# Mixture of experts on one core: four experts at a time with 32 token slots, weights in 8 KB pieces

## The chip, the cores and the metric

The kernel runs on one core of one Trainium2 chip. The metric is device time in microseconds (us), the median of three runs. TensorE (PE in the profile) multiplies matrices, VectorE (DVE) and ScalarE (ACT) do element-wise work and copies out of the accumulators (PSUM), SyncE (SP) issues the transfers, and 16 DMA engines carry them between the chip's memory and the on-chip memory (SBUF). 1 MB stands for 1,048,576 bytes where loads are counted; the profile's GB/s are 10^9 bytes a second.

## The reference

Two transformer blocks on 256 tokens of 1024 features, everything in float32. The change touches the last part only, a mixture of 32 experts in four groups of eight:

```
g_idx = argmax(xf @ w_router_group)                 # one of 4 groups for each token
top_logit, top_idx = top_k(local[g_idx], 2)         # two of the group's 8 experts
gate  = softmax(top_logit) * g_w                    # g_w: the group's softmax weight
hid   = silu(xblk @ w1[e]) * (xblk @ w3[e])         # w1, w3: 1024 x 512 for each expert
y    += gate * (hid @ w2[e])                        # w2: 512 x 1024 for each expert
out   = x + y                                       # xf, xblk: the tokens after an RMS norm
```

Each token goes to two experts, so there are 512 places over 32 experts. All 32 experts' weights are read: 32 x 3 x 2 MB = 192 MB. On the reference's own inputs the experts get between 4 and 32 tokens; the one with 32 is expert 27, and the token that comes closest to being the 33rd misses by 0.07 in a logit whose standard deviation is 4.8.

## The kernel before

The first five sixths of the program (two mixers, two feed-forwards, a gating unit and a cross attention) are not changed. For the experts the kernel routes the tokens first: it finds group and experts on VectorE, numbers the tokens of each expert (`rk`), and makes one-hot matrices (`select`, L1361) that map 128 slots to tokens: two experts with 64 slots (`CAP`) each.

The loop over pairs (L1532) then does, for each pair:

- `load_in` and `load_out` (L1394, L1409) ask for the pair's weights: 12 loads of 1 MB, each a slot of 128 partitions x 4 x 512 float32. A load takes four chunks of 128 rows, so each partition gets four separate rows of 2 KB.
- `hidden` (L1421): 8 steps over the 1024 features for w1 and then for w3; in each step one product for each expert, the expert's 64 slots as the stationary operand (64 columns of the PE array, the form 128*64 in the profile) and its weights as the moving one (512 columns). The program's product of float32 shows as two instructions in the trace.
- `gated` and `turned` (L1436, L1444): silu, product, and four transposes.
- the gather and the scatter matrix of the next pair (L1380, L1477), products of 128 x 128.
- `outputs` (L1453): products with w2, again 64 columns for each expert, a copy, and at L1457 the scatter back to the tokens, summed in PSUM over all experts.

The weights lie in 22 slots of 1 MB, used in turn (`slots`, L1320; `wslot`): 

```
slots[:] = [ra] * 4 + [rw] * 5 + [wp] * 2 + [cw] * 3 + [wp] * 4 + [(gp, "uh"), (gp, "ul"), rw, (cp, "h")]
```

A load waits until the last product that reads its slot is done, and for the load issued eight before it on the same queue: SP's is the only queue, and the framework keeps eight completion semaphores in turn. The order on each engine is made by a scheduler, except where `keep` pins it. The last pair loads in halves of 1 MB and cuts w2 into four column ranges, so that the end is short.

Two other loads serve below as a measure: at the program's start `u_row` (L502, L504) loads 128 rows of 1024 columns (4 KB each) and 128 rows of 2048 columns (8 KB each):

```
nc.sync.dma_start(wm[:, g, :], A["modT"][g, k * P:k * P + P, :])
nc.sync.dma_start(ws[k][:, 0, :], A["a_w_in"][k * P:k * P + P, 0:2048])
```

If an expert has more than `CAP` tokens, a loop behind a branch (L1568) runs over all experts again, once for each further `CAP` places up to 256.

Of the kernel before, what the change touches and what calls it, by code (L numbers as in the profile page):

```python
# [23 lines left out]
P = 128  # L24
# [7 lines left out]
CAP = 64  # L32

# the order in which some parts are interleaved, one letter for each step
WHOLE = (1, 5)  # rows of the first products for v and g that go in the tensor engine's exact float32
ROW_SEQ = ("rss", "srs", "srrs", "srs")  # layer 0: r the next row's norm, s the split of its weights
BAND_SEQ = ("m", "mm", "mm", "mm", "mm", "xx", "xx", "xx", "yyyy", "yyyx")  # m memory keys, x and y the output's halves
GATE_SEQ = "ghvut0123"  # the gating unit: see todo
CROSS_SEQ = "p1q0x1x21yyx3xy2y233"  # p and q the last queries, 0 to 3 a stage of a head, x and y the output's halves
GATHER_SEQ = (3, 1, 0, 0, 2, 1, 1, 1)  # the first experts: steps of the gather before and between those of w1  # L40
# [51 lines left out]
def _build(ctx, tc, nc, A, out, dbg):  # L92
# [17 lines left out]
    # ---------------------------------------------------------------- constants  # L110
# [41 lines left out]
    # ---------------------------------------------------------------- helpers  # L152
# [72 lines left out]
    def tick():  # L225
        """after each step of a product: a part of the previous one's epilogue, a share of the modulation rows"""
# [9 lines left out]
    def steps_t(w, u, ps, n=512, ks=range(KC)):  # L236
        """w 8 chunks [128, n] stationary, u (hi, lo) [128, 8, 256] moving -> n / 256 banks [128, 2, 256]"""
# [9 lines left out]
    def steps_n(w, u, ps, n=512, whole={}):  # L247
        """u (hi, lo) [128, 8, 256] stationary, w 8 chunks [128, n] moving -> 2 banks [128 tokens, n]"""
# [36 lines left out]
    def inv_rms(ss, n, w=T, eps=0, pool=None, keep=lambda i: i):  # L285
        """(ss / n + eps) ** -0.5 for ss [128, w] in PSUM: the table's value and a Newton step"""
# [43 lines left out]
    def put_u(u, k, src, gain, r, shift=None, keep=lambda i: i):  # L330
        """u[:, k] = src * gain * r + shift, as hi + lo"""
# [17 lines left out]
    # ---------------------------------------------------------------- modulation vectors  # L349
# [18 lines left out]
    def mod_queue(g, gain=None):  # L368
        """in steps for tick()"""
# [17 lines left out]
    def mod_done(g, gain=None):  # L387
        """bias; with a gain: gain * (1 + value)"""
# [7 lines left out]
    def residual(kk, ps, gate=None):  # L396
        """two feature chunks: h += ps * gate"""
# [15 lines left out]
    def norm(outs, adds):  # L413
        """outs: list of (gain(k), shift(k) or None, u)"""
# [5 lines left out]
    # ---------------------------------------------------------------- memory keys and values  # L420
# [22 lines left out]
    def mem_k_steps(hd):  # L443
        """the normalized memory keys of one head, transposed"""
# [17 lines left out]
    def mem_v(c, pool=pb):  # L462
        """256 columns of the memory values"""
# [15 lines left out]
    # ---------------------------------------------------------------- layer 0: HGRN2 mixer  # L479
    # The first norm and the products for f and q go by rows of the weights, each as soon as its modulation is there.  # L480
# [17 lines left out]
    def u_row(k):  # L498
        """the first norm's row k and the weights' row, in steps"""
# [22 lines left out]
    def w_split(n):  # L522
        """the n-th piece of the weights, 512 columns of row n // 4: f first; in steps"""
# [24 lines left out]
    with tc.tile_pool(name="hgrn", bufs=1, reuse_waits="tile") as hp:  # L548
        # lower bound: cumulative sum of the softmax over the single layer, less its first term
# [54 lines left out]
        def widen(lv, hf):  # L604
            """from level lv to level 2 lv"""
# [140 lines left out]
    # ---------------------------------------------------------------- feed-forward  # L746
# [51 lines left out]
    # ---------------------------------------------------------------- layer 1: chunk band attention  # L798
    with tc.tile_pool(name="band", bufs=1, reuse_waits="tile") as bp:
# [37 lines left out]
        def pair(j):  # L837
            """heads 2 j and 2 j + 1: the scores, the probabilities, the output"""
# [89 lines left out]
    # ---------------------------------------------------------------- second block: attention and gating unit  # L928
    with tc.tile_pool(name="blk2", bufs=1, reuse_waits="tile") as bp:
        # both norms at once: h / rms(h) * fin, and that over its own rms:  # L930
        # its mean square is mean(h^2 fin^2) / (mean(h^2) + eps), so that the two together are
        # h fin (mean(h^2 (fin^2 + eps)) + eps^2) ** -0.5
# [46 lines left out]
        def x1_update():  # L979
            """the residual stream enters this block through the first one's final norm"""  # L980
# [6 lines left out]
        def ug_steps():  # L987
            """the gating unit's u, transposed, and its g"""
# [25 lines left out]
        def pair(j):  # L1014
            """heads j and j + 4 of the queries, one for each key head"""
# [129 lines left out]
        # the rows of the attention's features first  # L1145
# [16 lines left out]
    # ---------------------------------------------------------------- memory cross attention  # L1162
# [19 lines left out]
    iota = kconst(mc, "iota")  # L1182
    rw = ctx.enter_context(tc.tile_pool(name="moe_r", bufs=6, side="right", reuse_waits="tile"))
# [17 lines left out]
    def head(hd):  # L1201
        """in three stages: the probabilities, these transposed, the output"""
# [61 lines left out]
    # the router's logits, tokens as rows, without the tokens' 1 / rms, which leaves the order of the experts as it  # L1264
    # is; the tokens themselves as rows, with the sums of their squares
# [65 lines left out]
    # its two experts: the other groups' logits count as -1e30  # L1331
# [13 lines left out]
    # the sum over the experts stays in PSUM, on top of the residual stream  # L1345
# [8 lines left out]
    # the place of each token in its experts' lists, from 1; 0 elsewhere  # L1354
# [5 lines left out]
    def select(es):  # L1360
        """[128 tok, 2, a pair of experts, CAP] one-hot"""  # L1361
        gsel = gp.tile([P, 2, 2, CAP], F32, tag="rms_v256", name=uid("gsel"))
        for tt in range(2):
            nc.vector.tensor_tensor(gsel[:, tt], rk[:, tt, es, None].to_broadcast([P, 2, CAP]),
                                    iota[:, None, 1:CAP + 1].to_broadcast([P, 2, CAP]), op=ALU.is_equal)
        return gsel

    gsel = select(slice(0, 2))
# [10 lines left out]
    # the tokens lack the norm so far: its gain comes to those gathered, 1 / rms to their products  # L1379
    def gather(gsel, g):  # L1380
        """the inputs of a pair of experts, in steps of g chunks"""
        xe = [gp.tile([P, 4, P], F32, tag="sq", name=uid("xe"), bufs=2) for _ in range(2)]
        yield [x[:, k, :] for x in xe for k in range(4)]
        for k0 in range(0, KC, g):
# [5 lines left out]
            for k in range(k0, k0 + g):  # L1390
                nc.scalar.activation(xe[k // 4][:, k % 4, :], ps[:, k - k0, :], AF.Copy, scale=col("nf2", k))
            yield

    def load_in(src, n=4):  # L1394
        """src(name, e): the weights w1 and w3 of a pair of experts, as 8 chunks [128, 512], n at a time"""
        w = {}
        for nm in ("w1", "w3"):
            for kh in range(2):
                ts = [wslot(512) for _ in range(2)]
                for k in range(0, 4, n):  # L1400
                    for e in range(2):
                        k0 = (4 * kh + k) * P
                        nc.sync.dma_start(ts[e][:, k:k + n, :], src(nm, e)[k0:k0 + n * P].rearrange("(k p) n -> p k n", p=P))
                for e in range(2):
# [4 lines left out]
    def load_out(src, cuts=(0, 512, D)):  # L1409
# [226 lines left out]
```

## Time and profile before

| | us |
|---|---|
| median of three runs (1391.45 to 1393.92) | 1392.39 |
| span of the profiled execution | 1390.3 |
| expert stage, from PE's first expert product (905.1) to the end | 485 |
| PE busy in the span | 1360.2 (98%) |
| DMA queue of SP, share of 16 engines' span | 82.0% |
| moved | 408.20 MB, mean 294 GB/s |

The span runs from the first to the last instruction of the profiled execution. That execution's time beyond its span is not in the profile; the median of the runs is 2.1 us above the span, and this is taken as what lies around it. A busy PE is an engine that has matmuls in flight, not one at its peak. The DMA share is the time that packets took on 16 engines; it can go a little over 1, since packets overlap.

### The profile page before, as it was taken

How to read it: one execution, taken by the hardware profiler on the slowest of the kernel's cores; microseconds unless marked ns; L12 is line 12 of the kernel's file. 1: busy time of each engine (PE TensorE's matmuls, PEld its weight loads, DVE VectorE, ACT ScalarE, POOL GpSimd, SP SyncE). 2: the span in 40 equal slices, each digit the busy share in tenths (PEclk: the TensorE clock that was granted, in tenths of full speed). 3: DMA queues.
4: the chain of work that ended last, by engine and by line, in shares of the span. 5: the costliest groups of instructions: out<-in, count | busy, mean ns of one | idle time of the engine just before them, and what ended most of it. 6: DMA issues, size and time to landing. Idle time of an engine off the chain costs nothing. (4 is left out here: it accounts for less than half of the span.)

```text
span 1390.3 us, 24824 instructions
## 1 busy us (share of the span) xinstructions
PE 1360.2 (98%) x9800; PEld 1046.7 (75%) x9800; DVE 734.3 (53%) x1597; ACT 609.2 (44%) x1276; POOL 11.9 (1%) x36
## 2 busy tenths in 40 slices
PE   7999899999999999999999999999999999999997
PEld 6967899999989789999998899954445444445443
DVE  7999998888897767555578777410000000000000
ACT  6756474555665656555577666421111111111111
POOL 2000000000000000000000000000000000000000
PEclk9999999999999999999999999999999999999999
DMA  9958889999878368554154278899999999999997
GB/s 370 377 193 296 284 307 331 328 341 346 316 260 317 124 214 260 188 193 156 62 160 158 72 273 309 291 333 386 387 387 386 386 387 387 387 387 386 387 386 251
DMA packets 219898, 408.20 MB, mean 294 GB/s; under 512 B 9985, under 2 KB 77825, under 8 KB 218754
## 3 DMA queue, kind: packets, MB, share of 16 engines
q1 hardware_dynamic: 219778, 406.58, 82.0%
q8 instruction: 78, 1.28, 0.4%
q14 instruction: 42, 0.34, 0.1%
HBM read 403.39 MB, written 3.15 MB: 292 GB/s over the span
## 5 line engine op out<-in xcount | busy, mean ns | idle before, releaser
L191 ACT ACTIVATE whi<-w 128x512 fp32r<-128x512 f32 (+1 forms) x448 | 277.7, 626 | 234.5 <-PE ps L197 113.9
L192 DVE TENSOR_TENSOR wlo<-w,whi 128x512 fp32r<-128x512 f32 (+1 forms) x448 | 298.6, 682 | 103.9 <-ACT whi L191 103.2
L1428 PE MATMUL r<-w,xe 128*64 128x512 f32 x1024 | 227.4, 596 | 0.0
L198 PE MATMUL ps<-uh,wlo 128*128 128x256 f32 x768 | 216.0, 282 | 1.7 <-DVE wlo L192 1.5
L197 PE MATMUL ps<-ul,whi 128*128 128x256 f32 x768 | 215.7, 281 | 0.5 <-DVE ul L340 0.5
L196 PE MATMUL ps<-uh,whi 128*128 128x256 f32 x768 | 215.6, 281 | 0.0
L1441 DVE SCALAR_TENSOR_TENSOR hs<-r,sc,hs 128x512 f32<-128x512 f32 (+1 forms) x17 | 12.1, 719 | 353.3 <-PE r L1428 353.0
L1428 PEld LDWEIGHTS r<-w,xe 128*64 128x64 f32 x1024 | 70.3, 137 | 136.6 <-issue 133.6
L196 PE MATMUL acc<-uh,whi 128*128 128x256 f32 x592 | 167.4, 289 | 4.7 <-ACT uh L515 4.3
L198 PE MATMUL acc<-uh,wlo 128*128 128x256 f32 x592 | 166.1, 284 | 0.8 <-DVE wlo L192 0.8
L197 PE MATMUL acc<-ul,whi 128*128 128x256 f32 x592 | 166.6, 283 | 0.0
L198 PEld LDWEIGHTS ps<-uh,wlo 128*128 128x128 f32 x768 | 144.5, 188 | 3.1 <-DVE wlo L192 3.1
L197 PEld LDWEIGHTS ps<-ul,whi 128*128 128x128 f32 x768 | 144.7, 188 | 0.7 <-DVE ul L340 0.7
L196 PEld LDWEIGHTS ps<-uh,whi 128*128 128x128 f32 x768 | 144.7, 188 | 0.0
L366 DVE SCALAR_TENSOR_TENSOR mt<-mt,cb 128x1024 f32<-128x1024 f32 x96 | 116.7, 1218 | 23.0 <-DMA mt<-in_modT 23.0
L196 PEld LDWEIGHTS acc<-uh,whi 128*128 128x128 f32 x592 | 110.7, 190 | 8.5 <-ACT uh L515 5.3
L1468 PE MATMUL r<-w,hT 128*64 128x512 f32 (+1 forms) x544 | 113.9, 570 | 0.1
L198 PEld LDWEIGHTS acc<-uh,wlo 128*128 128x128 f32 x592 | 111.7, 189 | 2.1 <-DVE wlo L192 1.2
L197 PEld LDWEIGHTS acc<-ul,whi 128*128 128x128 f32 x592 | 112.2, 190 | 1.3 <-issue 1.0
L196 PE MATMUL acc<-hh,whi 128*128 128x256 f32 x352 | 98.4, 279 | 0.0
L198 PE MATMUL acc<-hh,wlo 128*128 128x256 f32 x352 | 98.3, 279 | 0.0
L197 PE MATMUL acc<-hl,whi 128*128 128x256 f32 x352 | 98.1, 279 | 0.0
(343 smaller groups left out, 1940.9 us busy)
## 6 DMA issues: line engine op xcount, KB each, us to landing
w<-in_w SPq DMA_DIRECT2D x180, 1024.0 KB, 14.2
mt<-in_modT SPq DMA_DIRECT2D x96, 512.0 KB, 5.6
w<-in_ffn_w_in SPq DMA_DIRECT2D x88, 512.0 KB, 5.8
w<-in_ffn_w_out SPq DMA_DIRECT2D x22, 1024.0 KB, 8.4
w<-in_a_w_in SPq DMA_DIRECT2D x16, 1024.0 KB, 9.0
w<-in_w SPq DMA_DIRECT2D x24, 512.0 KB, 11.1
w<-in_modT SPq DMA_DIRECT2D x16, 512.0 KB, 9.0
w<-in_kv_w SPq DMA_DIRECT2D x8, 1024.0 KB, 7.7
```

Source lines behind the costliest of these rows:

```text
L191: keep(nc.scalar.activation(hi, raw, AF.Copy))
L192: keep(nc.vector.tensor_sub(lo, raw, hi.bitcast(F32)))
L196: nc.tensor.matmul(o, lh, rh, start=first, stop=False, skip_group_check=True)
L197: nc.tensor.matmul(o, lh, rl, start=False, stop=False, skip_group_check=True)
L198: nc.tensor.matmul(o, ll, rh, start=False, stop=last, skip_group_check=True)
L366: keep(nc.vector.scalar_tensor_tensor(w, w, 1.0, cb, op0=ALU.mult, op1=ALU.mult, accum_out=modr[:, g, j:j + 1]))
L1428: keep(nc.tensor.matmul(hps[i][e * 64:e * 64 + 64, :], xe[k][:, e * 64:e * 64 + 64], w[nm, e, k], start=k == 0, stop=k == KC - 1))
L1441: nc.vector.scalar_tensor_tensor(hs[:, o:o + n], hps[1][:, o:o + n], rs, hs[:, o:o + n], op0=ALU.mult, op1=ALU.mult)
L1468: keep(nc.tensor.matmul(yp[e * 64:e * 64 + 64, :], hT[:, c, e * 64:e * 64 + 64], w[e, o // 512, c][:, o % 512:o % 512 + n], start=c == 0, ...
```

## The change

Experts are taken four at a time (`G = P // CAP` = 4) with 32 slots each, so that the loop has 8 passes and not 16; each product with weights has 32 stationary columns in place of 64 (form 128*32). Each load of w1 and w3 now takes 512 consecutive rows of an expert, four consecutive rows (8 KB) to a partition; w2 comes in two loads of 1 MB for each expert, two whole rows of 1024 (8 KB) to a partition. So that the products still match, the features are dealt to the partitions in the same way: the token rows are copied with a stride of four (`row_copy`), the gate's output is written so too (`gated`), and the norm's gain comes in that order from `nf2p`, 8 new loads of 32 x 4 single values. The last group loads w1 and w3 as 4 KB pieces and w2 in three column ranges instead of four (2 KB, 1 KB and 1 KB pieces). Comments and docstrings are gone, and lines are numbered anew.

```diff
-CAP = 64
+CAP = 32
+G = P // CAP
+LAST_CUTS = (0, 512, 768, D)
...
+    nf2p = mc.tile([P, KC], F32, name="nf2p")
+    for half in range(2):
+        for q in range(4):
+            src = A["cols"]
+            nc.sync.dma_start(nf2p[32 * q:32 * q + 32, 4 * half:4 * half + 4],
+                              bass.AP(tensor=src.tensor, offset=src.offset + COLS["nf2"][0] + 4 * half + q,
+                                      ap=[[4 * NCOL, 32], [NCOL, 4]]))
...
-        nc.scalar.activation(xg[half, tt], rows[half, tt], AF.Copy)
+        nc.scalar.activation(xg[half, tt].rearrange("t (j p) -> t j p", j=4),
+                             rows[half, tt].rearrange("t (p j) -> t j p", j=4), AF.Copy)
...
-                ts = [wslot(512) for _ in range(2)]
+                ts = [wslot(512) for _ in range(G)]
                 for k in range(0, 4, n):
-                    for e in range(2):
-                        k0 = (4 * kh + k) * P
-                        nc.sync.dma_start(ts[e][:, k:k + n, :], src(nm, e)[k0:k0 + n * P].rearrange("(k p) n -> p k n", p=P))
-                for e in range(2):
+                    for e in range(G):
+                        rows = src(nm, e)[kh * 512:kh * 512 + 512].rearrange("(p k) n -> p (k n)", p=P)
+                        nc.sync.dma_start(ts[e].rearrange("p k n -> p (k n)")[:, k * 512:(k + n) * 512], rows[:, k * 512:(k + n) * 512])
+                for e in range(G):
...
+        if not cuts:
+            for s in range(2):
+                for e in range(G):
+                    t = wslot(D)
+                    rows = src("w2", e).rearrange("(p c) n -> p (c n)", p=P)
+                    nc.sync.dma_start(t.rearrange("p c n -> p (c n)"), rows[:, s * 2 * D:(s + 1) * 2 * D])
+                    for c in range(2):
+                        for half in range(2):
+                            w[e, half, 2 * s + c] = t[:, c, half * 512:half * 512 + 512]
...
-                for e in range(2):
-                    keep(nc.tensor.matmul(hps[i][e * 64:e * 64 + 64, :], xe[k][:, e * 64:e * 64 + 64],
+                for e in range(G):
+                    s = slice(e * CAP, e * CAP + CAP)
+                    keep(nc.tensor.matmul(hps[i][s, :], xe[k][:, s],
                                           w[nm, e, k], start=k == 0, stop=k == KC - 1))
...
-        nc.scalar.activation(hs, hps[0], AF.Silu, scale=rs)
-        for o in range(0, 512, n):
-            nc.vector.scalar_tensor_tensor(hs[:, o:o + n], hps[1][:, o:o + n], rs, hs[:, o:o + n], op0=ALU.mult, op1=ALU.mult)
+        h1, h3 = (x.rearrange("s (p c) -> s c p", c=4) for x in hps)
+        hc = hs.rearrange("s (c p) -> s c p", c=4)
+        nc.scalar.activation(hc, h1, AF.Silu, scale=rs)
+        for o in range(0, 4, n // P):
+            c = slice(o, o + n // P)
+            nc.vector.scalar_tensor_tensor(hc[:, c, :], h3[:, c, :], rs, hc[:, c, :], op0=ALU.mult, op1=ALU.mult)
...
-    for e0 in range(0, NE, 2):
-        last = e0 == NE - 2
-        cuts = (0, 256, 512, 768, D) if last else (0, 512, D)
+    for e0 in range(0, NE, G):
+        last = e0 == NE - G
+        cuts = LAST_CUTS if last else (0, 512, D)
         w = load_in(weights(e0), 2 if last else 4)
-        w2 = load_out(weights(e0), cuts)
+        w2 = load_out(weights(e0), cuts if last else ())
```

On PE, at the first expert products of the stage, before (`gsel`, `xg`: the gather; `w`, `xe`: weights and gathered tokens; `r`: an accumulator):

```order
L1388 MATMUL r_11543<-gsel_11519,xg_11456 128x128
L1388 MATMUL r_11543<-gsel_11519,xg_11458 128x128
L1428 MATMUL r_11589<-w_11565,xe_11533 64x512
L1428 MATMUL r_11589<-w_11566,xe_11533 64x512
L1388 MATMUL r_11593<-gsel_11519,xg_11456 128x128
L1388 MATMUL r_11593<-gsel_11519,xg_11458 128x128
```

and at the same place after:

```order
L1400 MATMUL r_11552<-gsel_11528,xg_11465 128x128
L1400 MATMUL r_11552<-gsel_11528,xg_11467 128x128
L1451 MATMUL r_11622<-w_11574,xe_11542 32x512
L1451 MATMUL r_11622<-w_11575,xe_11542 32x512
L1451 MATMUL r_11622<-w_11576,xe_11542 32x512
L1451 MATMUL r_11622<-w_11577,xe_11542 32x512
L1400 MATMUL r_11628<-gsel_11528,xg_11465 128x128
L1400 MATMUL r_11628<-gsel_11528,xg_11467 128x128
```

A step over the features reads four weight tiles where it read two, and each product writes 32 rows of the accumulator and not 64; the gather's steps stand between the same places.

On SP, ahead of the stage, before (`wr`: the router's weights; `mk`: keys of the cross attention):

```order
L142 DMA k_iota_10675<-in_consts 128x65
L1185 DMA wr_10680<-in_wr 128x8x40
L1403 DMA w2036_11573<-in_w3 128x4x512
L1403 DMA w2037_11574<-in_w3 128x4x512
L1403 DMA w2038_11577<-in_w3 128x4x512
L1171 DMA mk1941_11078<-memk_d_125 128x512
```

and after:

```order
L144 DMA k_iota_10675<-in_consts 128x33
L1190 DMA nf2p_10677<-in_cols 32x4x1 x8
L1195 DMA wr_10689<-in_wr 128x8x40
L1416 DMA w2036_11582<-in_w1 128x2048
L1416 DMA w2037_11583<-in_w1 128x2048
L1173 DMA mk1941_11087<-memk_d_125 128x512
```

The eight small loads stand ahead of the router's weights and of the fifth load of experts' weights; a load of experts' weights has one piece of 2048 values to a partition where it had four of 512.

On DVE, where the router's weights are multiplied by the norm's gain (`cqT`: the cross attention's queries; `r`, `t`, `v`: their norm; `wlo`: the split of a weight), before:

```order
L293 SCALAR_TENSOR_TENSOR r_10847<-t_10849,r_10847 128x256
L1186 TENSOR_TENSOR wr<-wr,cols 128x8x40
L1198 SCALAR_TENSOR_TENSOR cqT<-acc_10690,cq_10684,r_10847 128x256 x2
L291 TENSOR_TENSOR t_10881<-r_10879 128x256
L192 TENSOR_TENSOR wlo_10971<-w_10822,whi_10970 128x512
```

and after:

```order
L194 TENSOR_TENSOR wlo_11003<-w_10831,whi_11002 128x512
L1208 SCALAR_TENSOR_TENSOR cqT<-acc_10700,cq_10693,r_10888 128x256
L1196 TENSOR_TENSOR wr<-wr,cols 128x8x40
L1208 SCALAR_TENSOR_TENSOR cqT<-acc_10700,cq_10693,r_10888 128x256
L1220 TENSOR_REDUCE mx_10947<-s_10948 128x1
```

The product of the router's weights has moved from ahead of one head's two query products to between those of the next head.

## Rows read from the trace of the kernel before

**Rows 1.** The page's slices: busy tenths of PE, then GB/s, 40 slices.
```profile
PE   7999899999999999999999999999999999999997
...
GB/s 370 377 193 296 284 307 331 328 341 346 316 260 317 124 214 260 188 193 156 62 160 158 72 273 309 291 333 386 387 387 386 386 387 387 387 387 386 387 386 251
```
**Rows 2.** Busy time by stretch: header names the columns, last two DMA share and GB/s.
```profile
core 0: us, PE busy (x) PEld busy (x) DVE busy (x) ACT busy (x) POOL busy (x), PEclk, DMA share, GB/s
10.00:40.00 30.00, 25.73 (x199) 24.98 (x198) 27.76 (x57) 17.69 (x39) 1.56 (x1) 1.00 1.02 416
...
945.00:1355.00 410.00, 410.00 (x2132) 195.49 (x2130) 26.91 (x80) 65.18 (x168) 0.00 (x0) 1.00 1.05 386
1360.00:1370.00 10.00, 10.00 (x50) 3.16 (x44) 0.00 (x0) 0.69 (x1) 0.00 (x0) 1.00 1.06 363
...
1380.00:1390.30 10.30, 3.42 (x22) 2.15 (x18) 0.69 (x1) 1.23 (x3) 0.00 (x0) 0.86 0.23 80
```
**Rows 3.** Timeline of one pair: start us, us, engine, line, operation, count.
```profile
1102.70 2.05 PE L1388 MATMUL r<-gsel,xg 128*128 128x128 f32 x16
...
1107.53 7.09 PE L1468 MATMUL r<-w,hT 128*64 128x512 f32 x32
...
1116.47 1.94 PE L1428 MATMUL r<-w,xe 128*64 128x512 f32 x8
...
1120.27 12.24 PE L1428 MATMUL r<-w,xe 128*64 128x512 f32 x56
...
1132.43 2.05 PE L1388 MATMUL r<-gsel,xg 128*128 128x128 f32 x16
```
**Rows 4.** Waits from 850 us on, then SP's own from 945 to 1355: us, times, longest.
```profile
PEld r L1428 <- DMA w<-in_w: 1.7, 6, 0.3
...
SPq L1403 <- PE r L1428: 60.1, 36, 4.5
SPq L1416 <- PE r L1428: 26.4, 13, 5.2
```
**Rows 5.** Loads by tensor: count, KB each, median us from issue to landing.
```profile
w<-in_w SPq DMA_DIRECT2D x180, 1024.0 KB, 14.2
...
w<-in_a_w_in SPq DMA_DIRECT2D x16, 1024.0 KB, 9.0
w<-in_w SPq DMA_DIRECT2D x24, 512.0 KB, 11.1
w<-in_modT SPq DMA_DIRECT2D x16, 512.0 KB, 9.0
```
**Rows 6.** Line 1403, loads of w1 and w3: time from issue to landing.
```profile
DMA to landing us min/median/max: 5.3/14.1/16.8
```
**Rows 7.** Timeline where loads first wait for PE: steps 1 to 3, and SP.
```profile
906.79 2.80 PE L1428 MATMUL r<-w,xe 128*64 128x512 f32 x12
...
909.61 0.92 SPq L1416 DMA_DIRECT2D w<-in_w  x2
```
**Rows 8.** Timeline of the end: last cut of w2, scatter, copy.
```profile
1379.55 1.95 PE L1468 MATMUL r<-w,hT 128*64 128x256 f32 x16
...
1381.42 1.99 PE L1457 MATMUL acc<-sc,ys 128*128 128x256 f32 x8
```
**Rows 9.** Groups by form, one of 32 stationary columns: count, busy us, mean ns, idle.
```profile
L629 PE MATMUL ps<-qx,kd 128*32 128x64 f32 x128 | 2.8, 222 | 0.0
```
**Rows 10.** Timeline of SP and DVE at the router's weights, then copies of rows.
```profile
841.07 0.43 SPq L1185 DMA_DIRECT2D wr<-in_wr  x1
...
846.27 0.49 DVE L1186 TENSOR_TENSOR wr<-wr,cols 128x320 f32<-128x320 f32 x1 [1.15 <-DMA wr<-in_wr]
...
849.80 0.48 DVE L1198 SCALAR_TENSOR_TENSOR cqT<-acc,cq,r 128x256 f32<-128x256 f32 x1
...
899.35 1.08 ACT L1290 ACTIVATE xg<-xg 128x512 f32<-128x512 f32 x2 [2.79 <-PE xg L1278]
...
903.71 1.50 PE L1388 MATMUL r<-gsel,xg 128*128 128x128 f32 x12
```

More of the change, by code (lines that the diff above doesn't have):

```diff
@@ L1360, in select @@
     def select(es):
-        gsel = gp.tile([P, 2, 2, CAP], F32, tag="rms_v256", name=uid("gsel"))
+        gsel = gp.tile([P, 2, G, CAP], F32, tag="rms_v256", name=uid("gsel"))
         for tt in range(2):
-            nc.vector.tensor_tensor(gsel[:, tt], rk[:, tt, es, None].to_broadcast([P, 2, CAP]),
-                                    iota[:, None, 1:CAP + 1].to_broadcast([P, 2, CAP]), op=ALU.is_equal)
+            nc.vector.tensor_tensor(gsel[:, tt], rk[:, tt, es, None].to_broadcast([P, G, CAP]),
+                                    iota[:, None, 1:CAP + 1].to_broadcast([P, G, CAP]), op=ALU.is_equal)
         return gsel
-    gsel = select(slice(0, 2))
+    gsel = select(slice(0, G))
     lgg = small("lgg", 8, bufs=1).rearrange("p (t e) -> p t e", t=2)
@@ L1390, in gather @@
             for k in range(k0, k0 + g):
-                nc.scalar.activation(xe[k // 4][:, k % 4, :], ps[:, k - k0, :], AF.Copy, scale=col("nf2", k))
+                nc.scalar.activation(xe[k // 4][:, k % 4, :], ps[:, k - k0, :], AF.Copy, scale=nf2p[:, k:k + 1])
             yield
@@ L1407, in load_in, with load_out @@
         return w
-    def load_out(src, cuts=(0, 512, D)):
+    def load_out(src, cuts=()):
         w = {}
+        if not cuts:
[7 more added lines that the diff above has]
+                            w[e, half, 2 * s + c] = t[:, c, half * 512:half * 512 + 512]
         for o, o2 in zip(cuts, cuts[1:]):
             if o % 512 == 0:
-                ts = [wslot(512) for _ in range(2)]
-            for e in range(2):
-                nc.sync.dma_start(ts[e][:, :, o % 512:o % 512 + o2 - o], src("w2", e)[:, o:o2].rearrange("(k p) n -> p k n", p=P))
+                ts = [wslot(512) for _ in range(G)]
+            for e in range(G):
+                nc.sync.dma_start(ts[e][:, :, o % 512:o % 512 + o2 - o], src("w2", e)[:, o:o2].rearrange("(p c) n -> p c n", p=P))
                 for c in range(4):
@@ L1426, in hidden @@
             for k in range(KC):
-                for e in range(2):
-                    keep(nc.tensor.matmul(hps[i][e * 64:e * 64 + 64, :], xe[k][:, e * 64:e * 64 + 64],
+                for e in range(G):
+                    s = slice(e * CAP, e * CAP + CAP)
+                    keep(nc.tensor.matmul(hps[i][s, :], xe[k][:, s],
                                           w[nm, e, k], start=k == 0, stop=k == KC - 1))
@@ L1458, in scatter @@
                                       start=False, stop=last, skip_group_check=True))
-            if done and o2 % 256 == 0:
-                done(o2 // 256 - 1)
+            if done:
+                for kk in range(o // 256, o2 // 256):
+                    done(kk)
         after = None
@@ L1466, in outputs @@
             for c in range(4):
-                for e in range(2):
-                    keep(nc.tensor.matmul(yp[e * 64:e * 64 + 64, :], hT[:, c, e * 64:e * 64 + 64],
+                for e in range(G):
+                    s = slice(e * CAP, e * CAP + CAP)
+                    keep(nc.tensor.matmul(yp[s, :], hT[:, c, s],
                                           w[e, o // 512, c][:, o % 512:o % 512 + n], start=c == 0, stop=c == 3))
@@ L1477, in scatter_matrix @@
     def scatter_matrix(gsel, es):
-        gwt = gp.tile([P, 2, 2, CAP], F32, tag="rms_t256", name=uid("gwt"))
+        gwt = gp.tile([P, 2, G, CAP], F32, tag="rms_t256", name=uid("gwt"))
         for tt in range(2):
-            nc.vector.tensor_mul(gwt[:, tt], gsel[:, tt], gw[:, tt, es, None].to_broadcast([P, 2, CAP]))
+            nc.vector.tensor_mul(gwt[:, tt], gsel[:, tt], gw[:, tt, es, None].to_broadcast([P, G, CAP]))
         tp = ring([P, T + 1])
@@ L1531, in _build @@
     after = None
-    for e0 in range(0, NE, 2):
-        last = e0 == NE - 2
-        cuts = (0, 256, 512, 768, D) if last else (0, 512, D)
+    for e0 in range(0, NE, G):
+        last = e0 == NE - G
+        cuts = LAST_CUTS if last else (0, 512, D)
         w = load_in(weights(e0), 2 if last else 4)
-        w2 = load_out(weights(e0), cuts)
+        w2 = load_out(weights(e0), cuts if last else ())
         if e0 == 0:
             hps = hidden(w, xe, feed, GATHER_SEQ[1:])
-            sc, rs = scatter_matrix(gsel, slice(0, 2))
+            sc, rs = scatter_matrix(gsel, slice(0, G))
         else:
@@ L1546, in _build @@
         else:
-            es = slice(e0 + 2, e0 + 4)
+            es = slice(e0 + G, e0 + 2 * G)
             gsel = select(es)
@@ L1570, in _build @@
             nc.vector.tensor_scalar_add(rk, rk, -float(CAP))
-            with tc.For_i(0, NE, 2) as e0:
-                gsel = select(ds(e0, 2))
+            with tc.For_i(0, NE, G) as e0:
+                gsel = select(ds(e0, G))
                 xe, *_ = gather(gsel, 4)
-                sc, rs = scatter_matrix(gsel, ds(e0, 2))
+                sc, rs = scatter_matrix(gsel, ds(e0, G))
                 wcount[0] = 0
```

## The prediction

> **What bounds the kernel now.** I read the slices first [rows 1]: from about 870 us PE is full to the end and the rate of the DMA settles at 386 to 387 GB/s, more than anywhere before except the first slices. The stretches sharpen that [rows 2]: from 945 to 1355 us PE has matmuls in flight all the time at a granted clock of 1.00, and the DMA engines are full too (share 1.05). So two things could be the bound, and the waits and the timeline have to tell which.
>
> The timeline of a pair [rows 3] repeats: its first gather starts at 1102.70 and the next pair's at 1132.43, a period of 29.73 us. Products with w1 and w3 take 1.94 + 12.24 = 14.2 us of it, those with w2 7.1 us; some 8.5 us are gathers, transposes and scatters. A pair is 12 loads of 1 MB, 12.58 MB, and at 386 GB/s these need 32.6 us. PE is thus the faster by 2.9 us a pair, and lives on a stock: 22 slots are filled before PE's first product frees one, and the stock shrinks by about a MB a pair. The waits agree [rows 4]: after 850 us PE waits 1.7 us for weights, while SP waits far longer for PE to give slots back (60.1 + 26.4 us on its first two causes). At the very end both run out together: the last cut of w2 is multiplied from 1379.55 [rows 8], when the last loads land. Neither bound can be moved alone to any use: a faster PE would end on the loads, faster loads on PE.
>
> **The change: PE.** A group of four has the same number of steps as a pair, with four products to a step instead of two. In the pair's 64-column form two streams of 512 columns go at once: 64 instructions of w1 and w3 in 14.2 us are 0.22 us for one. If four narrow streams go at once too, a group costs PE what a pair costs, 29.7 us, and 8 groups 238 us instead of 476. The form 128*32 stands in the trace [rows 9]: 128 instructions of 64 columns in 2.8 us. A single stream runs at 2 x 0.22 us for 512 columns, so 64 columns take it 55 ns, and 128 of them 7.0 us: at least 2.5 went at once. With that width a group's products take 4 x 21.3 / 2.5 = 34 us and the group 43 us. I take 4 streams, and keep 2.5 as the other end.
>
> **The change: loads.** 180 + 24/2 = 192 loads of 1 MB [rows 5] stay; only the pieces grow, from 2 KB to 8 KB. Of those the trace has the program's start: from 10 to 40 us the loads are modT (4 KB pieces) and a_w_in (8 KB), equal in bytes, and they flowed at 416 GB/s with a share of 1.02 [rows 2]. Two equations for one engine of 16: eight pieces of 2 KB take 8 x 2048 x 16 / 386 = 679 ns, one of 8 KB and two of 4 KB take 16384 x 16 / 416 = 630 ns. The same bytes in 3 pieces instead of 8 save 49 ns, so a piece costs 9.8 ns beside its bytes; then 8 KB pieces flow at 422 GB/s, 4 KB at 410, 1 KB at 346. These are estimates from two rows; the bounds are 416 (the mixture as it is) and 434 (no cost per piece). A group's 24 MB need 59.6 us at 422, more than PE's 30 to 43: the stage becomes one of loads alone.
>
> **The sum.** Everything up to the first steps of the stage stays. At 909.61 [rows 7] SP issues the 23rd load, as soon as step 3 (x12, to 909.6) has freed the first slots; 170 loads are left. In the change that step frees four slots instead of two, and step 7 four more, so the queue does not run dry again. The first load needs 5.3 us to land on an empty queue [rows 6], 2.8 more than its bytes at 422. Then 146 MB of 8 KB pieces at 422 take 363 us, the last group's 16 MB of 4 KB pieces 41 us, 4 MB of 2 KB 10.9 us and 4 MB of 1 KB 12.1 us (the mixture of 1360 to 1370 ran at 363 GB/s [rows 2]): 427 us. The loads end at 909.6 + 2.8 + 427 = 1339.4, where before they end about 1379.
>
> What follows the last load now takes 1390.3 - 1379.55 = 10.8 us: 1.95 of products, 1.99 of scatter [rows 8], then copy, output and the program's end. The change has the same number of steps there, with 4 experts side by side: 10.8 again. But PE will have waited for most of the 22 us in which the last w2 arrives, and it was granted 0.86 on average over 1380 to 1390.3, in which it worked for 3.42 us and stopped [rows 2], so the clock falls to the lower of its two levels after work stops. At 1.2 instead of 2.4 GHz products and scatter take 3.9 us more, which I count. The span comes to 1339.4 + 10.8 + 3.9 = 1354.1.
>
> Small things. The eight nf2p loads stand ahead of the router's weights; at 0.43 us an issue [rows 10] these come 3.4 us later, and DVE waited 1.15 us for them as it is. Their product now stands on DVE near the query product of 849.80 instead of at 846.27, 3.5 us later, which covers it. If the single values land slowly DVE stands still with the queries and their norms behind it and PE waits for these; bounds 0 and +4 us, and I take +1. The strided copies of rows (two in 1.08 us from 899.35) have until 903.71, when the gather that reads them starts: were they twice as long they would still be done. The strided silu and product lie behind the loads of w2 in every group. So 1355.1, and with the 2.1 us between the span and the median of runs **1357 us**, 35 less than 1392.4.
>
> **The rivals.** First, 8 KB pieces may bring less than the two rows say; all of the gain hangs on it. Were they as slow as 2 KB pieces, 162 of the 170 MB would take 440 us instead of 404 and the time would be 1357 + 36 = 1393, no gain at all, since the loads then end where they end now. Against it stands 416 GB/s over 30 us; for it, that this was a short stretch with half 4 KB pieces, with other tensors. At 410 it is 1357 + 11 = 1368.
>
> The Trainium skill has a rule that speaks against the size: "DMA: Bandwidth & Descriptors", section "Why small descriptors are slow (HBM only)", puts about three cycles of fixed overhead on a packet that moves 32 bytes a cycle. By that 2 KB would cost 67 cycles for 64 and 8 KB 259 for 256, and 8 KB would flow at an estimated 399 GB/s, for 1378 us in all. The trace disagrees: its mixture of 4 and 8 KB already moved 416.
>
> Second, the clock. With gaps between bursts PE may stay at 1.2 GHz, and a group would then take 2 x 29.7 = 59.4 us of PE, level with the 59.6 of its loads; every wait would add, and the time would come back to between 1375 and 1395. For it: a burst of 4 steps is 3.4 us of work in the 10 us in which 4 MB land. Against it: at half clock PE is hardly idle, and the trace shows 1.00 wherever PE is kept busy [rows 2]. The Trainium skill ("TensorE: Matmul & The Clock Gate", section "Why this matters for your kernels") asks for matmuls without idle gaps for the same reason. By that rule the bursts are at risk, and no run here shows yet how long they stay slow.
>
> Third, slower than before: the narrow products don't overlap. One at a time, a group's products take 4 x 21.3 = 85 us and the group 94, 750 in all where there were 476: 1392 + 274 = 1666 us. It decides from the point where fewer than 85 / (59.5 - 8.5) = 1.7 go at once. The 2.5 of [rows 9] stand against it, on short products only.
>
> Last, the change may not do what it says: one expert holds exactly 32 tokens. Were it 33 by the kernel's own rounding, the loop behind the branch would run 7 times over all weights, 7 x 477 us at 422 GB/s, some 3300 us more. The nearest token is 0.07 of a logit away, far beyond float32 rounding.
>
> **How the numbers follow.** The forecast (1349 to 1363) gets 0.64; smaller gain by the pieces (1363 to 1389) 0.17; faster than 1349, by a warm end or a rate near 430 (146 MB at 430 save 7 us) 0.09; the slow clock 0.06; the narrow products 0.03 and the loop 0.01. Range 1344 to 1375: it leaves out the slow half of the small gain, the clock and the slower cases. About 0.2% can be told from no change: faster 0.92, same 0.04 (the rate of 2 KB, or the clock), slower 0.04.
>
> **What would show it.** Right: from about 950 us to the end of loads GB/s near 422, PE waiting for loads in the tens of us a group, SP no longer waiting for PE, products of four experts starting together and 4 steps in 3.4 us at full clock. Wrong: a rate of 386 to 400; or SP still waiting for PE while the granted clock is 0.5; or steps that take 1.7 us at a clock of 1.00.

## The result and the profile after

| | before | after |
|---|---|---|
| median of four runs, us | 1392.06 | 1354.63 (1352.67 to 1356.54) |
| span of the profiled execution, us | 1390.3 | 1354.8 (that execution: 1356.54) |
| ratio | | 0.9731, 95% interval 0.9718 to 0.9744 |

The change makes the kernel 37 us faster; 1357 was forecast. The profiled execution is the slowest of the four. The page of the kernel after, busy tenths of PE and then GB/s in 40 slices:

```profile
PE   6999899999999999999999999999777787768786
...
GB/s 365 382 183 311 263 325 344 328 315 354 334 245 329 147 134 282 227 187 186 124 63 203 94 149 274 303 296 417 421 421 421 421 421 421 421 419 422 417 409 273
```

Where [rows 1] has a full PE beside 386 GB/s, PE is now at seven tenths beside 421. The stretches, with the columns of [rows 2]:

```profile
945.00:1280.00 335.00, 258.56 (x1428) 86.46 (x1426) 11.08 (x32) 26.70 (x70) 0.00 (x0) 0.90 1.01 421
1280.00:1300.00 20.00, 17.84 (x111) 6.26 (x110) 0.00 (x0) 1.19 (x2) 0.00 (x0) 1.00 1.02 409
1320.00:1330.00 10.00, 6.92 (x22) 1.31 (x22) 0.88 (x2) 0.77 (x2) 0.00 (x0) 1.00 1.04 387
1330.00:1340.00 10.00, 8.11 (x46) 1.88 (x50) 0.00 (x0) 0.60 (x1) 0.00 (x0) 0.66 1.09 354
```

The DMA engines are full to about 1340, and the rate falls with the pieces: 8 KB to 1280, 4 KB, 2 KB and last a mixture with 1 KB. PE has work in flight for 258.6 of 335 us, at a mean granted clock of 0.90, and stands still for the rest.

The waits of the weight loads and products on PE from 850 to 1355 us (us, times, longest of one):

```profile
PEld r L1451 <- DMA w<-in_w: 117.3, 77, 2.4
...
PEld r L1497 <- DMA w<-in_w: 63.1, 33, 2.7
```
```profile
PE r L1451 <- DMA w<-in_w: 54.4, 57, 1.5
PE r L1497 <- DMA w<-in_w: 31.7, 29, 1.8
```

and those of SP from 945 to 1320:

```profile
SPq L1416 <- DMA w<-in_w: 207.0, 112, 2.5
SPq L1430 <- DMA w<-in_w: 99.1, 47, 3.0
SPq L1430 <- PE r L1451: 3.1, 9, 0.4
```

The picture of [rows 4] is turned round. There PE's weight loads waited 1.7 us and SP stood 60.1 + 26.4 us for PE; now the weight loads wait 180 us and the products behind them 86 us, and SP waits for the load eight before its own, which is to say for the DMA engines. A load of line 1416 takes 19.8 us from issue to landing (14.1 in [rows 6]): eight in flight at 2.49 us each.

```profile
w<-in_w SPq DMA_DIRECT2D x172, 1024.0 KB, 19.8
```

PE's timeline (start, us, operation, count; in brackets the idle time ahead and what ended it), at steps 1 to 3, in a later group and at the end:

```profile
908.53 1.07 PE L1451 MATMUL r<-w,xe 128*32 128x512 f32 x8
...
910.17 2.78 PE L1451 MATMUL r<-w,xe 128*32 128x512 f32 x24
...
1096.33 1.05 PE L1497 MATMUL r<-w,hT 128*32 128x512 f32 x2 [1.44 <-DMA w<-in_w]
1098.84 1.91 PE L1497 MATMUL r<-w,hT 128*32 128x512 f32 x2 [1.46 <-DMA w<-in_w]
...
1339.42 1.91 PE L1497 MATMUL r<-w,hT 128*32 128x256 f32 x26 [0.30 <-DMA w<-in_w]
1341.27 1.99 PE L1484 MATMUL acc<-sc,ys 128*128 128x256 f32 x8
1343.19 1.24 PE L1497 MATMUL r<-w,hT 128*32 128x256 f32 x6
1345.20 1.91 PE L1497 MATMUL r<-w,hT 128*32 128x256 f32 x26 [0.77 <-DMA w<-in_w]
1347.05 1.99 PE L1484 MATMUL acc<-sc,ys 128*128 128x256 f32 x8
```

Three steps of four products take 2.78 us, what three steps of two took in [rows 7]: four narrow products run at once. Later each expert's first product waits 1.4 us for its own load, one load after another, 2.5 us apart. The last one arrives at 1345.20, and 9.6 us later the program is over.

### The profile page after: what moved, and what is told of

Its sections match the earlier page's. It is cut to its first block, busy times and chain, and to the rows that moved or that the text cites. A ratio compares the mean times of both kernels' runs of the same rounds, so it can differ in the third digit from the quotient of the medians.

```text
span 1354.8 us, 23674 instructions
## 1 busy us (share of the span) xinstructions
PE 1238.6 (91%) x9336; PEld 941.9 (70%) x9336; DVE 719.8 (53%) x1549; ACT 572.7 (42%) x1179; POOL 12.2 (1%) x36
## 4 chain that ended last, share of the span: by engine, by line
PE 57%; DMA 32%; DVE 7%; ACT 1%; SPq 1%; issue 1%; POOL 0%; DVEq 0%; ACTq 0%; POOLq 0%
DMA w<-in_w 30%; PE acc L200 9%; PE acc L199 9%; PE acc L198 9%; PE ps L200 7%; PE ps L199 7%; PE ps L198 7%; DVE wlo L194 2%; DMA mt<-in_modT 1%; PE ss L324 1%; PE r L1451 1%; DVE ut L335 1%; DVE mt L368 1%; SPq L1438 1%; PE po L881 1%
## 5 line engine op out<-in xcount | busy, mean ns | idle before, releaser
L1451 PE MATMUL r<-w,xe 128*32 128x512 f32 x1024 | 188.3, 672 | 54.6 <-DMA w<-in_w 54.4
L1468 DVE SCALAR_TENSOR_TENSOR hs<-r,sc,hs 128x512 f32<-128x512 f32 (+1 forms) x9 | 6.1, 690 | 349.3 <-PE r L1451 348.9
L1451 PEld LDWEIGHTS r<-w,xe 128*32 128x32 f32 x1024 | 40.3, 119 | 190.1 <-DMA w<-in_w 117.3
L1497 PE MATMUL r<-w,hT 128*32 128x512 f32 (+1 forms) x544 | 96.7, 654 | 31.9 <-DMA w<-in_w 31.7
## 6 DMA issues: line engine op xcount, KB each, us to landing
w<-in_w SPq DMA_DIRECT2D x172, 1024.0 KB, 19.8
```

What stands on the lines that cost most here:

```text
L1451: keep(nc.tensor.matmul(hps[i][s, :], xe[k][:, s], w[nm, e, k], start=k == 0, stop=k == KC - 1))
L1497: keep(nc.tensor.matmul(yp[s, :], hT[:, c, s], w[e, o // 512, c][:, o % 512:o % 512 + n], start=c == 0, stop=c == 3))
```

## The experiments

Theory: behind the first products the stage is bound by the loads alone. Its length is the bytes by a rate that the size of the pieces sets; four narrow products at once only keep PE below that line. Neither half of the change is worth anything by itself. The rivals are that one half earns the gain alone, that the rate comes from something other than the pieces, and that the narrow products run 2.5 at a time.

**The same kernel again**, no edit, as the measure for its neighbours.

> The changed kernel once more, as the measure for its neighbours: 1354.6 +-2 us. Its first profile reached the expert stage 3.4 us later than before did (first expert product at 908.5 instead of 905.1), and PE had fallen behind at 455 to 465 us, where its granted clock was 0.70 and 0.62 instead of 1.00, in a part that the change leaves alone. Theory A: this is chance of one execution; another profile has the clock at 1.00 there, its first expert product near 905, and a span some 3 us shorter. Theory B: it comes with the changed program (its instructions ahead of there stand in another order); the profile shows the same fall of the clock and 908.5 again.

Measured: 1355.65 us (1353.0 to 1357.61), span 1352.6. The profile of 455 to 465 us, first of the first execution, then of this one:

```profile
455.00:460.00 5.00, 3.07 (x9) 1.73 (x9) 3.43 (x20) 3.61 (x16) 0.58 (x4) 0.70 0.37 102
460.00:465.00 5.00, 5.00 (x22) 3.63 (x20) 1.92 (x9) 1.60 (x8) 0.29 (x2) 0.62 0.09 26
```
```profile
455.00:460.00 5.00, 4.58 (x27) 3.19 (x28) 4.00 (x25) 3.67 (x16) 0.59 (x4) 1.00 0.35 107
460.00:465.00 5.00, 5.00 (x33) 3.48 (x32) 2.72 (x12) 3.42 (x15) 0.29 (x2) 1.00 0.18 52
```

In the first execution PE stood still for two of five microseconds, and its clock was partly at the lower level then and just after; in the second it kept working and stayed at full clock. So the fall does not come with the changed program each time. Where the delay arises can be read from one group of products: at 446 us the two traces of the kernel before and the two of the change stand within 0.03 us of each other, and the last start in this group is

```profile
L879 PE MATMUL po<-pT,v x32: 379/404/431, 457.9 to 504.6; 128*64 128x256 f32 x32
```
```profile
L881 PE MATMUL po<-pT,v x32: 379/430/689, 459.7 to 508.3; 128*64 128x256 f32 x32
```

504.6 before and 508.3 in the first execution after; in this second one it is 506.3. The later start of the stage thus arises in these 60 us, 400 us ahead of it. The first expert product stood at 906.63, not 905: theory A is right on the clock, but 1.5 us of delay are there at full clock too, and their cause stays open.

**The kernel before again**, no edit.

> The kernel before once more, for one more profile of it. Open: its first expert product stood at 905.14 us; in nine profiles of kernels with the change or a part of it this product (the first of L1428, after L1451) stands between 905.9 and 910.6, also without the gain's loads, and the granted clock fell at 455 to 465 us in two of them. Theory A (the place varies from execution to execution, in before too): a first product somewhere between 905 and 908.5, with waits of PE at 455 to 465 us that differ from the first profile. Theory B (the changed program itself starts its stage 1 to 2 us later): 905.1 again, within 0.3 us. The time, 1390 to 1394 us, tells nothing.

Measured: 1392.63 us (one run); the first expert product at 905.75, 0.6 us off its first profile. Neither theory is borne out in full: the place moves in before too, but by less than the 1 to 2 us in question, and two profiles cannot settle that. The group of products above ends its starts at 504.8 here, and in the kernels with the change or a part of it between 504.6 (pieces of 4 KB, below) and 509.8: the change does not have to bring the delay; whether it makes it likelier stays open.

**PE's half alone: groups of four, 2 KB pieces.**

```diff
-rows = src(nm, e)[kh * 512:kh * 512 + 512].rearrange("(p k) n -> p (k n)", p=P)
-nc.sync.dma_start(ts[e].rearrange("p k n -> p (k n)")[:, k * 512:(k + n) * 512], rows[:, k * 512:(k + n) * 512])
+k0 = (4 * kh + k) * P
+nc.sync.dma_start(ts[e][:, k:k + n, :], src(nm, e)[k0:k0 + n * P].rearrange("(k p) n -> p k n", p=P))
...
-w2 = load_out(weights(e0), cuts if last else ())
+w2 = load_out(weights(e0), cuts)
```

> The half of the change that PE sees, alone: groups of four with 32 slots, three column ranges in the last group, but every load in the old layout of 2 KB pieces (features in the old order, so the loads of the gain go too). Theory (both bounds of before ran out together; with a faster PE the loads remain, at 386 GB/s): PE waits for loads from some 40 us into the stage on; of the 170 MB behind the first freed slots 166 at 386 and 4 at 354 GB/s take 463 us, as against 427; 1355 + 36 = 1390 us, the time of before. Rival (what gained was PE's work, the pieces are a side matter): 1355 us, or at 4 KB's rate 1363.

Measured: 1389.82 us, ratio 0.9971 (0.9959 to 0.9982). The stage, and PE's wait for the last range at the end:

```profile
945.00:1355.00 410.00, 310.07 (x1594) 99.83 (x1586) 11.08 (x32) 28.62 (x73) 0.00 (x0) 0.88 1.05 387
```
```profile
1378.30 1.91 PE L1489 MATMUL r<-w,hT 128*32 128x256 f32 x26 [0.80 <-DMA w<-in_w]
```

PE, busy through all of the 410 us before, is now busy for 310 of them, and the end has not moved but for 3 us: the last load is awaited until 1378.3, where before it was 1379.55 [rows 8], because the rate is still 387. The rival, 1355 or 1363, is out.

**The loads' half alone: pairs with 64 slots, 8 KB pieces.**

```diff
-CAP = 32
+CAP = 64
```

> The other half alone: pairs with 64 slots, each load in 8 KB pieces, the rest as in the change. Theory (PE has 29.7 us of work in a pair, whose 12 MB at 421 GB/s would be there in 29.9 us): PE stays full, 485 us from its first expert product to the end as before; a rate of some 421 GB/s only while slots are free, SP waits for PE; 1388 to 1393 us, no gain that can be told. Rival 1 (what gained were the loads): 1355 us. Rival 2 (loads at 386 GB/s held PE back more than its 1.7 us of waits show, through late slots): 1370 to 1380 us.

Measured: 1392.48 us, ratio 1.0001 (0.9986 to 1.0016). Stretches, and SP's waits from 945 to 1355 us:

```profile
1000.00:1280.00 280.00, 280.00 (x1444) 132.86 (x1442) 17.82 (x54) 42.67 (x110) 0.00 (x0) 1.00 1.01 421
...
1340.00:1360.00 20.00, 20.00 (x112) 10.22 (x110) 1.18 (x2) 3.96 (x11) 0.00 (x0) 1.00 0.47 160
```
```profile
SPq L1416 <- PE r L1497: 111.6, 13, 9.3
SPq L1416 <- PE r L1451: 95.6, 38, 2.6
```

The loads run at 421 and are through by 1360, but PE never stands still in these stretches and ends when it did: from its first expert product (910.55) to the end of the span (1394.6) are 484 us, before 485. Both rivals are out. Both halves thus bring 3 and 0 us apart and 37 together. That is what two bounds that lie side by side look like.

**Pieces of 4 KB.** The 1 MB loads of the change in two pieces to a partition; features and gain are dealt to match.

```diff
-rows = src(nm, e)[kh * 512:kh * 512 + 512].rearrange("(p k) n -> p (k n)", p=P)
+rows = src(nm, e)[kh * 512 + k * P:kh * 512 + (k + n) * P].rearrange("(j p k) n -> p j (k n)", p=P, k=2)
...
-rows = src("w2", e).rearrange("(p c) n -> p (c n)", p=P)
-nc.sync.dma_start(t.rearrange("p c n -> p (c n)"), rows[:, s * 2 * D:(s + 1) * 2 * D])
+rows = src("w2", e)[s * 256:s * 256 + 256].rearrange("(c p) n -> p c n", p=P)
+nc.sync.dma_start(t, rows)
```

> Groups of four as in the change, the same 1 MB loads, but each in two pieces of 4 KB to a partition instead of one of 8 KB. Theory (the stage after 913 us is bound by the loads alone, and a piece costs 9.8 ns beside its bytes): 409 to 410 GB/s from 945 us to the end of the whole loads, where the change has 421; the 146 MB that were in 8 KB pieces need 374 instead of 364 us, so 1365 us. Rival 1 (a fixed cost of each piece plays no part, and 2 KB pieces were slow for another reason): 421 GB/s and 1355 us. Rival 2 (each packet costs about three cycles, by the Trainium skill, DMA: Bandwidth & Descriptors, Why small descriptors are slow (HBM only); an estimate): a step of only 1.2% from 8 to 4 KB, 416 GB/s and some 1359 us.

Measured: 1363.05 us (1361.54 to 1366.4), 7.4 more than its neighbour with 8 KB.

```profile
945.00:1280.00 335.00, 253.06 (x1402) 85.94 (x1398) 11.08 (x32) 26.69 (x70) 0.00 (x0) 0.89 1.03 409
```

The rate is 409, as the theory has it. For one engine of 16, 16 KB take 16384 x 16 / 421 = 623 ns in two pieces, 641 ns at 409 in four and 677 ns at 387 in eight: 9 ns for each further piece, both times. Rival 1 is out. The time came out 2 us under the theory's 1365; its first expert product stood at 906.5. Rival 2, an estimate from the packet cost that the Trainium skill states ("DMA: Bandwidth & Descriptors", section "Why small descriptors are slow (HBM only)"), has 1.2% between 4 and 8 KB; the runs show 2.9%, and they decide.

Another rival was not named ahead: that SP's issues set the rate, since a load in two pieces holds SP for 2.3 us here:

```profile
L1417 SPq DMA_DIRECT2D w<-in_w x144: 327/2300/4708, 809.1 to 1320.5; - x144
```

The change itself speaks against it: from 1280 to 1300 us its loads are single pieces of 4 KB, issued in 0.33 us each, and they flow at the same 409.

**PE's own time.** A third of the loads for the first seven groups, all of PE's instructions.

```diff
-w = load_in(weights(e0), 2 if last else 4)
-w2 = load_out(weights(e0), cuts if last else ())
+w = load_in(weights(e0), 2 if last else 4, ("w1", "w3") if last else ("w1",))
+if last: w2 = load_out(weights(e0), cuts)
+else: w["w3", e, k] = w["w1", e, k]; w2[e, half, c] = w["w1", e, 4 * half + c]   # for all e, k, half, c
```

> PE's own time in the change: the first seven groups load only w1 (8 MB of 24) and use its tiles for w3 and w2 too, so 112 MB of loads are left out and their products are of other numbers; all of PE's instructions stay. Theory (four narrow products run at once): 29.7 us a group at a granted clock of 1.00, 8 groups 238 us, from the first expert product near 906 to a span of 1150 to 1158, and PE waits for loads only in the last group. Rival 1 (2.5 at once): 43 us a group, 1255 us. Rival 2 (the clock stays at 1.2 GHz whatever the loads do, the products overlap): 59 us a group, 1385 us.

Measured: 1158.03 us (one run), span 1156.3. One group in the timeline of PE:

```profile
1089.39 1.92 PE L1451 MATMUL r<-w,xe 128*32 128x512 f32 x16
...
1093.17 12.22 PE L1451 MATMUL r<-w,xe 128*32 128x512 f32 x112
...
1110.15 7.08 PE L1497 MATMUL r<-w,hT 128*32 128x512 f32 x64
...
1119.08 1.50 PE L1451 MATMUL r<-w,xe 128*32 128x512 f32 x12
```

The period is 1119.08 - 1089.39 = 29.69 us, to be laid beside the 29.73 of a pair in [rows 3]: 1.92 + 12.22 us for twice as many products. Where PE does not wait for weights its clock is 1.00 all the while:

```profile
945.00:1130.00 185.00, 185.00 (x1568) 82.86 (x1564) 11.09 (x32) 28.58 (x73) 0.00 (x0) 1.00 0.72 284
```

Both rivals are out. The lower clock of the stage in the change is thus a consequence of PE's waits. I count it as free, since PE's group, 29.7 us at full clock, has 59.8 us of loads beside it; no run took it away alone.

By these numbers PE needs some 166 of the 335 us from 945 to 1280 (an estimate, 335 x 29.7 / 59.8), and yet it is busy for 258.6 in the change. There an expert's products often go alone, while the other experts' loads are still on their way: two instructions take 1.05 us at 1096.33, where eight of four experts took 1.07 at 908.53. So the seven tenths of the page do not say how near PE is to being the bound.

**Eighteen slots in place of 22.**

```diff
-... + [cw] * 3 + [wp] * 4 + [(gp, "uh"), (gp, "ul"), rw, (cp, "h")]
+... + [cw] * 3 + [wp] * 4
```

> The change with 18 slots of 1 MB instead of 22. Theory (the end is the first freed slots plus what is then left to load at the rate, plus the tail): 4 MB more are left at 421 GB/s, 4 x 2.49 = 10 us later, 1365 us. Rival 1 (the stock only hides jitter; the stage is bound by how PE frees slots): 1355 us. Rival 2 (with fewer than 24 slots for the 24 loads of a group the queue starves, since a whole step of four frees at once): a rate below 415 GB/s in the stage and more than 1372 us.

Measured: 1361.66 us (1358.45 to 1363.07): 6 us more than the change with 22, not 10. What the theory had wrong is the count. The edit takes four entries from the list but only three buffers from the memory: the entry `rw` draws from a pool of six, which is as large as before and is used in turn by five entries. So 4 + 6 + 6 + 3 = 19 buffers are left (`ra`, `rw`, `wp`, `cw`). The trace agrees: ahead of the first expert product SP issues 16 loads at line 1416, and at line 1430 six with 22 slots (first line, the change run again) and three here:

```profile
L1430 SPq DMA_DIRECT2D w<-in_w x6: 327/328/436, 881.4 to 905.4; - x6
```
```profile
L1430 SPq DMA_DIRECT2D w<-in_w x3: 327/328/328, 882.7 to 901.7; - x3
```

Three buffers are 3 x 2.49 = 7.5 us by the theory's own rule. The last range's products start at 1351.84 here and at 1343.17 in the change run again, 8.7 us apart, of which 1.2 are a later start of the stage (907.87 and 906.63): 7.4 are left. Afterwards the loads run at 421 as in the change:

```profile
945.00:1280.00 335.00, 256.02 (x1420) 86.31 (x1412) 11.08 (x32) 26.73 (x70) 0.00 (x0) 0.90 1.01 421
```

So the stock is worth its bytes at the rate here: each MB that is not loaded ahead of the first products ends the loads some 2.5 us later. Rivals 1 and 2 are out.

**Without the gain's eight loads.**

```diff
-scale=nf2p[:, k:k + 1]
+scale=col("nf2", k)
```

> The change without its eight loads of 32 x 4 single values: the gathered tokens are multiplied by the gain in its old order (so the gains no longer match the permuted features). Theory: these loads delay the router's weights by 6 us, and DVE's wait for them, 0.9 us, reaches nobody: 1354.6 +-1, the same as the change. Rival: the 3.4 us by which the stage starts later come from them: 1351.2 us, with the first expert product at 905 us.

Measured: 1354.96 us (1354.43 to 1357.92), its neighbour 1355.65; first expert product at 907.13. The loads cost nothing that can be told, and the later start of the stage is not theirs.

**Whole rows in the last group.**

```diff
-w = load_in(weights(e0), 2 if last else 4)
+w = load_in(weights(e0))
...
+# w2 of the last group: rows 0 and 1 of each partition as one 8 KB piece, row 2 as 4 KB, row 3 from cut to cut
+for c, o, o2 in [(2, 0, D)] + [(3, *x) for x in zip(cuts, cuts[1:])]:
+    for e in range(G):
+        nc.sync.dma_start(ts[e][:, c - 2, o:o2], src("w2", e).rearrange("(p c) n -> p c n", p=P)[:, c, o:o2])
...
+# the products with rows 0 to 2 for all ranges first, then row 3 range by range
```

> A version that may be better: the last group too loads w1 and w3 as 8 KB pieces (1 MB loads); of its w2 the first two rows of each partition come as one 8 KB piece, the third as one of 4 KB, and only the fourth in the three column ranges; PE makes all products with the first three rows for all ranges first. Theory (loads bound the end): the last 24 MB take, at 421, 409, 387 and 354 GB/s for 8, 4, 2 and 1 KB, 20 MB 49.8 + 2 MB 5.1 + 1 MB 2.7 + 1 MB 3.0 = 60.6 us instead of 63.8, and the last range has a quarter of its products left after the last load, 0.5 us instead of 1.9: 4.5 us less, 1350 us. Rival 1 (the end is bound by PE, whose clock is low there, or by the time from issue to landing of the many small loads): 1354 to 1357 us, no gain. Rival 2: only the 1.4 us of products behind the last load: 1353 us.

Measured: 1350.44 us (1348.16 to 1351.11), ratio to before 0.969 (0.9674 to 0.9706). None of its runs reaches the lowest of the change beside it (1353.0), so it beats both kernels. The end of the chain of waits (start, us, what):

```profile
1336.07 2.69 PE r L1492 x11
1338.76 1.94 PE acc L1483 x8
```

and PE's timeline there:

```profile
1333.70 5.07 PE L1492 MATMUL r<-w,hT 128*32 128x512 f32 x34 [0.23 <-DMA w<-in_w]
1338.69 1.99 PE L1483 MATMUL acc<-sc,ys 128*128 128x256 f32 x8
1340.62 0.64 PE L1492 MATMUL r<-w,hT 128*32 128x256 f32 x8
1341.18 1.99 PE L1483 MATMUL acc<-sc,ys 128*128 128x256 f32 x8
```

The last scatter begins at 1341.18; beside it, in the change run again, at 1345.01. Of these 3.8 us, 0.7 are an earlier start of the stage; the other 3.1 are about what was forecast for the loads alone, 3.2. The 1.4 us behind the last load did not show: PE's last products (1340.62) no longer wait for a load but for the scatter ahead of them, so PE ends the chain. The medians are 5.2 us apart, the spans 3.3; what lies between these is within the scatter of the runs.

## Why the prediction was right

Point by point, by its own steps.

**Both bounds together.** Right, and shown: PE's half alone 0.9971, the loads' half alone 1.0001, both 0.9731.

**PE at 29.7 us a group.** Right: 29.69 when loads are out of the way. The 2.5 at once of [rows 9] was too low an end: those short products did not show the width.

**422, 410 and 386 GB/s for 8, 4 and 2 KB.** Measured 421, 409 and 387; the mixture with 1 KB 354. The 9.8 ns for a piece, taken from a stretch of 30 us at the other end of the program, came out at 9. This was the term on which all hung, and the 4 KB run shows that it is the size of the pieces. Two slips did no harm: without a cost per piece the two rows give 436 GB/s and not 434, and 4 of the 16 steps in 14.2 us are 3.55 us and not 3.4.

**The start.** The sum had the loads end at 1339.4; the last range's products began at 1345.20. Of these 5.8 us 3.4 are the stage's later start (first expert product at 908.53, not 905.1). The sum took everything ahead of the stage as fixed, and it is not: that delay is already there at 508 us, part of it beside a fall of the clock, and the change run again stood 1.9 us earlier. The rates account for 0.6 us (427.3 in place of 426.7). About 1.1 us lie at the very end, where the sum had the engines full to the last byte and they were not:

```profile
911.00:917.00 6.00, 5.99 (x50) 2.51 (x43) 0.00 (x0) 1.10 (x3) 0.00 (x0) 1.00 0.65 239
1340.00:1344.00 4.00, 4.00 (x35) 2.21 (x26) 0.69 (x1) 0.98 (x2) 0.00 (x0) 1.00 0.80 257
```

Four microseconds at 257 in place of 354 are 1.1 us. The first line bears the queue's new start out: six microseconds at 239 in place of 421 are 2.6 us, where the sum had 2.8. The rest, some 0.9 us, I cannot place.

**The tail.** The failed step: "At 1.2 instead of 2.4 GHz products and scatter take 3.9 us more, which I count." Measured were 1354.8 - 1345.20 = 9.6 us and not 14.7. The clock did fall while PE waited for w2 (0.66 from 1330 to 1340), but the previous ranges' products and their scatter kept PE at work from 1339.4 on nearly without a gap, and the last range ran at full clock: 1.91 and 1.99 us, where [rows 8] has 1.95 and 1.99. Of the 5.1 us that the tail was counted too long, 3.9 are thus this clock; the other 1.2 lie behind the start of the last scatter (7.75 us to the end, before 8.9). So the tail was 5.1 us too long and the end of the loads 5.8 us too early, and the two nearly cancel. The span came out 0.3 us under the sum's 1355.1 for this reason; the closeness is partly luck, the mechanism is not.

**The gain's loads.** SP and DVE at that place:

```profile
844.89 5.81 SPq L1190 DMA_DIRECT2D nf2p<-in_cols  x8
850.74 0.59 SPq L1195 DMA_DIRECT2D wr<-in_wr  x1
```
```profile
853.42 0.49 DVE L1196 TENSOR_TENSOR wr<-wr,cols 128x320 f32<-128x320 f32 x1 [0.89 <-DMA wr<-in_wr]
```

Eight issues took 5.8 us on SP, not 3.4 as by the 0.43 of [rows 10]; DVE waited 0.89 us for the router's weights, less than the 1.15 before. The cost was counted as 1 us; the run without them shows none.

**The rivals.** Smaller gain: out by the rate. The slow clock: half right, since the mean granted clock was 0.90 with spells at the lower level in the waits, but PE had twice the time it needs. Narrow products that do not overlap: out. An expert with 33 tokens: out; the program ended behind the last group.

## What to carry to other kernels

When two engines are full at once, change both or neither: price each alone against the other's bound, and expect almost nothing until the second one moves. A rate for a piece size that the stage does not use may stand elsewhere in the same trace, and two such rows gave a cost per piece that carried over here (9.8 ns forecast, 9 measured). Count the buffers of a stock by what is filled ahead of the first product, not by the entries of a list. Where the loads are the bound, look last at what the end is cut into: small pieces there cost their rate, and the cuts that they buy are worth only what still waits for a load.

## What the hardware showed unexpectedly

A load in several pieces to a partition holds SP for long while the DMA engines are full. In the change the twelve w2 loads of the last group (four pieces of 2 or 1 KB) took 544 to 3171 ns each to issue, the loads of w1 and w3 (one piece of 8 or 4 KB) mostly 328:

```profile
L1438 SPq DMA_DIRECT2D w<-in_w x12: 544/1985/3171, 1313.6 to 1336.7; - x12
```
```profile
L1416 SPq DMA_DIRECT2D w<-in_w x144: 327/328/1301, 812.9 to 1312.3; - x144
```

It is no matter of the last group: before, the median for four pieces of 2 KB is 2526 ns, and with two pieces of 4 KB it is 2300. The issue by itself is not that long, since the shortest of before takes 367 ns. That it need not cost anything the 4 KB rate shows, the same 409 with either kind of issue; for the pieces of 1 and 2 KB no run took the hold away alone.
